# Slot weights without matmuls, four adaLN halves inside the router, one buffer for gathered rows and a 21st weight slot

## The chip, the core and the metric

The kernel runs on one core of a Trainium2 chip. The metric is the device time of one execution in microseconds, as the median of several runs. TensorE multiplies (its weight loads are counted apart, as PEld), VectorE and ScalarE do elementwise work and empty PSUM, GpSimd does almost nothing here, and SyncE (SP) issues nearly all DMAs, the weights among them.

## What is computed

The kernel computes two layers of a decoder trunk for 256 tokens of width 1024 in float32. Each layer has a mixer and a mixture of experts, both modulated by adaLN vectors made from a conditioning vector:

```python
c_act = jax.nn.silu(c)
for l in range(2):
    mod = c_act @ ada_w[l] + ada_b[l]
    sh1, sc1, gt1, sh2, sc2, gt2 = jnp.split(mod, 6, axis=-1)
    h = modulate(rms_norm(x, norm1_g[l]), sh1, sc1)
    x = x + gt1 * token_mixer(h, ...)      # retention, FoX, MLA; gates; out_w
    h = modulate(rms_norm(x, norm2_g[l]), sh2, sc2)
    x = x + gt2 * hier_moe(h, ...)
return rms_norm(x, final_g)
```

`hier_moe` picks for each token the best of 4 groups and the two best of its 8 experts, and adds the two results `(silu(xb @ w1[e]) * (xb @ w3[e])) @ w2[e]`, each by its weight. There are 32 experts, w1 and w3 of 1024 x 512 and w2 of 512 x 1024 each.

## The kernel before

The tokens are two tiles of 128 (index `t`), the width is two halves of 512 (index `n`). All weights come from HBM in loads of 1 MB (128 x 2048 float32). `Ring` holds the plan: the loads in a fixed order, each given to the first free slot (`fill`), and since one queue (SP, L139) issues them all, a load that has no free slot holds up those behind it. `take` hands out a loaded slot, `give` returns it, `grow` adds slots that live in memory that only one stage needs. There are 12 main slots (`slot`); during the experts 20: also two in `more_right`, three in `more_left`, and three in the work area `ar` (offsets `A_MORE`), of which the last is added when the mixer has ended.

The **mixer** computes adaLN vectors (`ada`), attention and gates, and last the out projection (`out`, L179 in `mm` as all matmuls, L188 is a transpose). An adaLN half (512 of its columns) is one load and is computed either as 16 passes of matmuls (out<-in of 32 x 512) or by VectorE (L511, then one matmul from `acc`). The halves' places in the plan are spread over the mixer; the last `ADA_TAIL` = 2 stand at its end, behind the out weights. `out` ends with the router: for each half `n`, VectorE adds the residual (`residual`, L592 and L593), `router_half` transposes x (L188), ScalarE copies it (L1224), and matmuls of 128 x 36 sum the logits. Then the left pool is opened, the last slot is added, two adaLN halves are computed (`ADA_FIRST`), and `route` runs: a chain of small VectorE operations per tile (`choose`, from L1251 on), with small matmuls in between (`pulse`) that have no use but to keep TensorE going.

The **experts** (`moe`) are taken in 16 pairs, 64 rows for each of the two (`CAP`), which fill the two halves of the 128 rows. `gather` picks their tokens by a matmul with a one-hot (`wanted`, L1320), into one of two buffers. A pair then runs on TensorE in this order: w1 (32 matmuls in two parts, each taking two loads), `combine` of the pair before (8 matmuls that add its rows to the tokens), `slots_of` (two one-hots transposed, and two matmuls of 128 x 2 that give each row its weight `wsl`; VectorE copies both out, L1372 and L1373), w3, the gather of the next pair around four transposes of the hidden rows (copied by ScalarE, L1436), w2. Each w2 half is scaled by `wsl` into `yh` and `yl`. If any expert has more than 64 tokens, `overflow` computes the rest; the test is a register load and a branch ahead of pair 12. In the last pair `gate_rows` spreads the gate's vector (two matmuls, two copies L583), and in layer 1 `final_gain` does the same for the final gain, a half each in pairs 11 and 12.

## Time and profile before

| | us |
|---|---|
| median of 3 runs | 1554.18 (1547.79, 1554.18, 1554.46) |
| the profiled execution | 1548.13 |
| its span | 1546.5 |
| TensorE busy in it | 1468.5 (95%) |
| VectorE, ScalarE busy | 661.7 (43%), 447.9 (29%) |
[...]

The span goes from the first to the last instruction; the profiled execution has its own time, which stands nearer to the lowest of the three runs. Layer 0's experts run from about 328 to 770 us, layer 1's from 1076 to 1527. PE is a TensorE matmul, PEld its weight load, DVE VectorE, ACT ScalarE, SPq the queue of SyncE. A time in a row is in microseconds from the span's start unless it is a mean of nanoseconds.

### The profile page before, as it was taken

The page shows a single profiled execution, that of the slowest core. Times are in us where ns is not written, and L with a number is a line of the kernel's source. Part 1 is how long each engine was busy: PE and PEld are TensorE (multiplying, and loading weights), DVE is VectorE, ACT ScalarE, POOL GpSimd, SP SyncE. Part 2 cuts the span into 40 slices and gives each one's busy share as a digit, 9 for nine tenths or more (in the row PEclk, how much of TensorE's full clock was granted, in tenths as well). Part 3 has the DMA queues.
Part 4 walks back from the last instruction along what each step waited for, and adds up shares of the span by engine and source line. Part 5 has one row for each costly group of instructions (what it writes and reads, how often), then busy time and mean ns, then how long its engine had stood idle before and what let it go on. Part 6 is the DMA issues. An engine that isn't in the chain of part 4 may idle for free. (4 is left out here: it accounts for less than half of the span.)

```text
span 1546.5 us, 21205 instructions
## 1 busy us (share of the span) xinstructions
PE 1468.5 (95%) x8326; PEld 897.6 (58%) x8326; DVE 661.7 (43%) x1756; ACT 447.9 (29%) x897; POOL 6.0 (0%) x10
## 2 busy tenths in 40 slices
PE   6898999999999999999989989999999999999996
PEld 3776889854444444444458679897444444444442
DVE  3766697962222222122157669767222222222223
ACT  3554534431111111111154454454211121111112
POOL 0000000000000000000000000000000000000001
PEclk9999999999999999999999999999999999999998
DMA  9963477998999999999995546668999999999993
GB/s 385 384 231 136 152 270 270 371 379 365 421 420 421 421 421 421 420 420 420 411 366 191 220 148 261 243 243 322 385 420 421 420 420 421 421 420 419 422 416 124
DMA packets 78542, 535.16 MB, mean 346 GB/s; under 512 B 8608, under 2 KB 8864, under 8 KB 15968
## 3 DMA queue, kind: packets, MB, share of 16 engines
q1 hardware_dynamic: 77776, 532.89, 85.2%
q8 instruction: 69, 1.13, 0.3%
q10 hardware_dynamic: 656, 0.80, 0.1%
q14 instruction: 41, 0.34, 0.1%
HBM read 532.61 MB, written 1.05 MB: 345 GB/s over the span
## 5 line engine op out<-in xcount | busy, mean ns | idle before, releaser
L179 PE MATMUL bank<-slot,ar 128*64 128x512 f32 (+1 forms) x1876 | 453.6, 593 | 1.8 <-ACT ar L1436 1.5
L179 PEld LDWEIGHTS bank<-slot,ar 128*64 128x64 f32 (+1 forms) x1876 | 143.0, 137 | 253.9 <-issue 235.6
L255 DVE TENSOR_TENSOR ws<-slot,ws 128x512 fp32r<-128x512 f32 (+1 forms) x276 | 186.5, 682 | 104.8 <-ACT ws L253 97.6
L179 PE MATMUL bank<-hr,ws 128*128 128x256 f32 x1536 | 204.7, 289 | 8.4 <-DVE ws L255 7.3
L179 PE MATMUL bank<-ar 128*64 128x512 f32 (+3 forms) x692 | 209.2, 502 | 0.7 <-DVE ar L885 0.7
L179 PEld LDWEIGHTS bank<-hr,ws 128*128 128x128 f32 x1536 | 191.8, 193 | 19.2 <-DVE ws L255 10.0
L253 ACT CAST ws<-slot 128x512 fp32r<-128x512 f32 (+1 forms) x276 | 164.4, 619 | 101.9 <-PE bank L179 95.8
L179 PE MATMUL bank<-ws,hr 128*128 128x512 f32 (+1 forms) x576 | 152.7, 410 | 10.0 <-ACT ws L253 4.6
L1338 ACT ACTIVATE ar<-bank,GS 128x128 f32<-128x128 f32 x128 | 58.6, 458 | 355.1 <-PE bank L179 324.3
L179 PE MATMUL bank<-more_left,ar 128*64 128x512 f32 x456 | 137.6, 594 | 0.0
L179 PEld LDWEIGHTS bank<-ar,x 128*128 128x128 f32 x1024 | 119.2, 192 | 25.1 <-issue 21.1
L179 PE MATMUL bank<-ar,x 128*128 128x128 f32 x1024 | 128.3, 278 | 1.7 <-DVE ar L1320 1.5
L179 PEld LDWEIGHTS bank<-ws,hr 128*128 128x128 f32 x576 | 107.7, 193 | 37.7 <-ACT ws L253 6.4
L1455 DVE SCALAR_TENSOR_TENSOR yl<-bank,wsl,yh 128x512 fp32r<-128x512 f32 x60 | 45.0, 750 | 157.6 <-ACT yh L1454 156.6
L179 PEld LDWEIGHTS bank<-ar 128*64 128x64 f32 (+2 forms) x692 | 80.9, 155 | 45.9 <-issue 38.1
L1372 DVE COPY wsl<-bank 64x1 f32<-64x1 f32 x64 | 10.0, 156 | 227.7 <-PE bank L179 227.2
L1336 DVE TENSOR_SCALAR ar<-bank,GS 128x128 f32<-128x128 f32 x128 | 52.5, 410 | 115.8 <-ACT ar L1338 115.8
L1419 DVE TENSOR_TENSOR R<-R,bank 128x512 f32<-128x512 f32 x32 | 22.0, 688 | 178.5 <-PE bank L179 178.5
L511 DVE SCALAR_TENSOR_TENSOR acc<-slot,cz,acc 128x512 f32<-128x512 f32 x122 | 90.8, 744 | 0.1
L179 PEld LDWEIGHTS bank<-more_left,ar 128*64 128x64 f32 x456 | 41.0, 137 | 82.5 <-issue 76.3
L1454 ACT ACTIVATE yh<-bank,wsl 128x512 fp32r<-128x512 f32 x60 | 41.3, 688 | 151.2 <-PE bank L179 151.2
L179 PE MATMUL bank<-yr,ws 128*128 128x256 f32 x576 | 75.4, 286 | 2.4 <-DVE ws L255 2.2
(244 smaller groups left out, 1158.8 us busy)
## 6 DMA issues: line engine op xcount, KB each, us to landing
slot<-in_exp_w SPq DMA_DIRECT2D x226, 1024.0 KB, 19.8
ar<-in_exp_w SPq DMA_DIRECT2D x54, 1024.0 KB, 19.8
more_left<-in_exp_w SPq DMA_DIRECT2D x54, 1024.0 KB, 19.8
slot<-in_ada_w SPq DMA_DIRECT2D x46, 1024.0 KB, 6.6
more_right<-in_exp_w SPq DMA_DIRECT2D x38, 1024.0 KB, 19.4
slot<-in_w_in SPq DMA_DIRECT2D x24, 1024.0 KB, 9.7
slot<-in_gate_w SPq DMA_DIRECT2D x23, 1024.0 KB, 5.0
slot<-in_branch_w SPq DMA_DIRECT2D x12, 1024.0 KB, 4.7
```

The lines of the kernel that those rows point to most:

```text
L179: self.nc.tensor.matmul(out, lhsT, rhs, start=start, stop=stop, skip_group_check=True)
L253: self.nc.scalar.copy(hi, w)
L255: self.nc.vector.tensor_tensor(lo, w, hi.bitcast(F32), ALU.subtract)
L511: nc.vector.scalar_tensor_tensor(acc, v[:, t, :], c, acc, ALU.mult, ALU.add)
L1336: nc.vector.tensor_scalar(hgT[:, j], pv[:, i], G[:, j:j + 1], S[:, j:j + 1], ALU.mult, ALU.add)
L1338: nc.scalar.activation(hgT[:, j], pv[:, i], AF.Identity, bias=S[:, j:j + 1], scale=G[:, j:j + 1])
L1372: nc.vector.tensor_copy(wsl(p)[es], ps[es, 256 + e:257 + e])
L1419: nc.vector.tensor_tensor(hid, hid, G[1], ALU.mult)
L1454: nc.scalar.mul(self.yp[n][0], G[n], wsl(p))
L1455: nc.vector.scalar_tensor_tensor(self.yp[n][1], G[n], wsl(p), self.yp[n][0].bitcast(F32), ALU.mult, ALU.subtract)
```

## The change

- `slots_of` has no 128 x 2 matmuls any more. The one-hots carry the weights, so the transposed rows hold the weight where they held 1; VectorE sums a row for `wsl` and compares with zero for the one-hot `OT`.
- The gathered rows have one buffer instead of two, the transposed hidden rows lie in `R`, the one-hots in `acc`. The memory that this frees is a fourth `A_MORE` slot, the 21st, added after `route`.
- `ADA_TAIL` and `ADA_FIRST` go from 2 to 4: four adaLN halves stand at the end of the mixer's plan. They are all matmuls and are computed inside `out`, between the two router halves. So fewer halves are left to VectorE.
- One `pulse` is gone. The rows of the second gate are copied before pair 0's Silu.
- The overflow test stands ahead of pair 11 in layer 0 and 13 in layer 1. `final_gain` runs in pair 13 and in the last pair, behind `gate_rows`. What only an overflow needs is done inside its branch.

```diff
-A_RV, A_RQK, A_RG, A_QT, A_KT, A_ST, A_RB = 0, 1024, 2048, 3072, 3584, 4096, 4096
+A_RV, A_RQK, A_RG, A_QT, A_KT, A_ST = 0, 1024, 2048, 3072, 3584, 4096
-A_HG, A_MORE, A_HIDT, A_OH = (4864, 5888), (0, 2048, 6912), 4096, (4608, 8960)
+A_HG, A_MORE = (4096, 8960), (0, 2048, 6912, 4864)
-ADA_TAIL, ADA_FIRST = 2, 2
+ADA_TAIL, ADA_FIRST = 4, 4
-OVERFLOW = 12
+OVERFLOW = (11, 13)
...
-        self.ring.grow([self.v(o, 2048) for o in A_MORE[:2]], l)
+        self.more = {o: self.v(o, 2048) for o in A_MORE}
+        self.ring.grow([self.more[o] for o in A_MORE[:2]], l)
...
                     if n:
                         self.finish(half)
+                        while not self.parked:
+                            self.step(self.live)
+                        self.tail = True
+                        for _ in range(ADA_FIRST):
+                            next(ga, None)
                     half = self.router_half(n)
...
         run(out())
-        while not self.parked:
-            self.step(self.live)
         pool = self.open_extra(l, "left", 3)
...
-        self.ring.grow([self.v(A_MORE[2], 2048)], l)
-        self.tail = True
-        for _ in range(ADA_FIRST):
-            next(ga, None)
+        self.ring.grow([self.more[A_MORE[2]]], l)
         self.route()
+        self.ring.grow([self.more[A_MORE[3]]], l)
...
         tsc(o1, self.iota0, fi[:, 0:1], None, ALU.is_equal)
-        self.pulse(t, o1)
...
-    def one_hot(self, p, t, by=None):
+    def one_hot(self, p, t, by):
-        oh = self.v(A_OH[t] + 2 * CAP * (p % 2), 2 * CAP)
+        c = 256 * t + 2 * CAP * (p % 2)
+        oh = self.acc[:, 0, c:c + 2 * CAP]
...
-            if by is None:
-                self.nc.vector.tensor_scalar(o, self.iota1[:, 0:CAP], r, None, ALU.is_equal)
-            else:
-                self.nc.vector.tensor_scalar(o, self.iota1[:, 0:CAP], r, by, ALU.is_equal, ALU.mult)
+            self.nc.vector.tensor_scalar(o, self.iota1[:, 0:CAP], r, by(e), ALU.is_equal, ALU.mult)
...
     def moe(self, l):
-        hg = [self.v(o, 8, 128) for o in A_HG]
+        hgT = [self.v(A_HG[0] + 128 * j if j < 6 else A_HG[1] + 128 * (j - 6), 128) for j in range(8)]
         hid = self.R
-        hidT = self.v(A_HIDT, 4, 128)
+        hidT = hid.rearrange("p (a b) -> p a b", a=4)
...
         def slots_of(p):
             ps = S[2]
-            oh = [self.one_hot(p, t) for t in range(NT)]
             for t in range(NT):
-                self.tr(ps[:, 128 * t:128 * t + 128], oh[t])
-            for t in range(NT):
-                self.mm(ps[:, 256:258], oh[t], self.W[:, t, 2 * p:2 * p + 2], t == 0, t == 1)
-            for e in range(2):
-                es = slice(64 * e, 64 * e + 64)
-                nc.vector.tensor_copy(wsl(p)[es], ps[es, 256 + e:257 + e])
-            nc.vector.tensor_copy(self.OT, ps[:, 0:256])
+                self.tr(ps[:, 128 * t:128 * t + 128], self.one_hot(p, t, lambda e: self.W[:, t, e:e + 1]))
+            nc.vector.tensor_reduce(wsl(p), ps[:, 0:256], AX.X, ALU.add)
+            nc.vector.tensor_scalar(self.OT, ps[:, 0:256], 0.0, None, ALU.not_equal)
...
-            if p == OVERFLOW:
+            if p == OVERFLOW[l]:
                 combine(p - 1)
-                self.overflow(l)
-            hgT = hg[p % 2]
+                self.overflow(l, hgT, lambda: self.gather(wanted(p), hgT))
...
             if p == 0:
                 self.together(self.rest)
+                R, vec = self.rowsB
+                self.rowsB = self.acc[:R.shape[0], 1], vec
+                nc.scalar.copy(self.rowsB[0], R)
...
-            if l == DEPTH - 1 and OVERFLOW - 1 <= p <= OVERFLOW:
-                self.final_gain(p - (OVERFLOW - 1))
+            if l == DEPTH - 1 and p == OVERFLOW[l]:
+                self.final_gain(0)
             if p == 0:
-                R, vec = self.rowsB
-                self.rowsB = self.acc[:R.shape[0], 1], vec
-                nc.scalar.copy(self.rowsB[0], R)
...
             elif end:
-                self.together(self.gate_rows(12 * l + 10, A_HG[0], self.rowsB, S[2:4]))
+                o = next(o for o in A_MORE if any(self.more[o] is s for s in self.ring.free))
+                self.together(self.gate_rows(12 * l + 10, o, self.rowsB, S[2:4]))
+                self.y32 = self.v(o + 1024, 1024)
+                if l == DEPTH - 1:
+                    self.final_gain(1)
```

On TensorE in layer 1, from the last transposes of the router's first half to the start of the choice (`bank_69` collects the logits, `bank_70` the adaLN vectors; `cz` is the conditioning vector), before:

```order
L188 MATMUL bank_67<-cst,x 128x128 x4
L179 MATMUL bank_69<-cst,ar 128x36 x8
L188 MATMUL bank_64<-cst,x 128x128 x4
L188 MATMUL bank_65<-cst,x 128x128 x4
L179 MATMUL bank_69<-cst,ar 128x36 x8
L179 MATMUL bank_70<-slot_92,cz 32x512 x4
L179 MATMUL bank_70<-slot_89,cz 32x512 x4
L179 MATMUL bank_63<-cst,sm 4x128
```

and now:

```order
L188 MATMUL bank_67<-cst,x 128x128 x4
L179 MATMUL bank_69<-cst,ar 128x36 x8
L179 MATMUL bank_70<-ar,cz 32x512 x8
L179 MATMUL bank_70<-slot_90,cz 32x512 x4
L179 MATMUL bank_70<-slot_100,cz 32x512 x4
L188 MATMUL bank_64<-cst,x 128x128 x4
L188 MATMUL bank_65<-cst,x 128x128 x4
L179 MATMUL bank_69<-cst,ar 128x36 x8
L179 MATMUL bank_63<-cst,sm 4x128
```

Two halves that stood behind the second set of logits, and two more, stand ahead of the transposes that lead to it.

On SP in layer 1, the expert loads around the end of the mixer (the two rows of `ar` are the first `A_MORE` slots, `more_left` the left pool), before:

```order
L139 DMA slot_98<-in_exp_w 128x2048
L139 DMA slot_100<-in_exp_w 128x2048
L139 DMA ar<-in_exp_w 128x2048 x2
L139 DMA more_left_7358<-in_exp_w 128x2048
L139 DMA more_left_7359<-in_exp_w 128x2048
L139 DMA more_left_7360<-in_exp_w 128x2048
L139 DMA ar<-in_exp_w 128x2048
L139 DMA slot_92<-in_exp_w 128x2048
L139 DMA slot_89<-in_exp_w 128x2048
```

and now:

```order
L139 DMA slot_91<-in_exp_w 128x2048
L139 DMA slot_97<-in_exp_w 128x2048
L139 DMA ar<-in_exp_w 128x2048 x2
L139 DMA slot_90<-in_exp_w 128x2048
L139 DMA slot_100<-in_exp_w 128x2048
L139 DMA more_left_7346<-in_exp_w 128x2048
L139 DMA more_left_7347<-in_exp_w 128x2048
L139 DMA more_left_7348<-in_exp_w 128x2048
L139 DMA ar<-in_exp_w 128x2048 x2
```

The four slots ahead of the left pool are now those of the four adaLN halves, and behind the pool two loads go to `ar` instead of one.

On TensorE in a pair of layer 1, from the last matmul of a combine to w3 (`bank_69` takes the transposed one-hots, `bank_64` w3), before:

```order
L179 MATMUL bank_68<-yh_7364,OT 128x512
L179 MATMUL bank_68<-yl_7365,OT 128x512
L188 MATMUL bank_69<-cst,ar 128x128 x2
L179 MATMUL bank_69<-rt,ar 128x2 x2
L179 MATMUL bank_64<-slot_91,ar 64x512
```

and now:

```order
L179 MATMUL bank_68<-yh_7352,OT 128x512
L179 MATMUL bank_68<-yl_7353,OT 128x512
L188 MATMUL bank_69<-cst,acc 128x128 x2
L179 MATMUL bank_64<-more_left_7346,ar 64x512
L179 MATMUL bank_64<-more_left_7347,ar 64x512
```

The pair of matmuls from `rt`, which holds the weights, is gone.

## Rows read from the trace of the kernel before

**Rows 1.** The page's first part: busy us, share of the span, instructions.

```profile
PE 1468.5 (95%) x8326; PEld 897.6 (58%) x8326; DVE 661.7 (43%) x1756; ACT 447.9 (29%) x897; POOL 6.0 (0%) x10
```

**Rows 2.** Stretches: from:to, length, busy PE, PEld, DVE, ACT, POOL, clock, DMA share, GB/s.

```profile
1375.00:1400.00 25.00, 25.00 (x136) 12.08 (x136) 6.11 (x18) 4.28 (x8) 0.00 (x0) 1.00 1.01 420
...
321.50:390.50 69.00, 65.53 (x366) 33.11 (x367) 21.77 (x107) 14.68 (x30) 0.00 (x0) 0.95 0.95 390
...
1068.90:1133.40 64.50, 61.86 (x360) 31.35 (x360) 22.14 (x107) 15.79 (x33) 0.00 (x0) 1.00 0.97 399
...
341.40:348.30 6.90, 6.48 (x18) 2.68 (x20) 2.31 (x12) 0.48 (x1) 0.00 (x0) 0.51 1.00 411
```

**Rows 3.** The chain of waits, pairs 13 to 15 of layer 1: start, us.

```profile
1454.49 0.22 PE bank L188 x2
...
1482.35 0.22 PE bank L188 x2
...
1520.22 0.59 ACT ar L1436
```

**Rows 4.** Issues on SP, one load each: start, us, line.

```profile
314.67 0.33 SPq L139 DMA_DIRECT2D slot<-in_exp_w  x1
...
736.76 0.33 SPq L139 DMA_DIRECT2D slot<-in_exp_w  x1
...
1064.29 0.33 SPq L139 DMA_DIRECT2D ar<-in_exp_w  x1
...
1479.39 0.33 SPq L139 DMA_DIRECT2D slot<-in_exp_w  x1
```

**Rows 5.** The same four loads in that order: KB each, us from issue to landing.

```profile
slot<-in_exp_w SPq DMA_DIRECT2D x1, 1024.0 KB, 6.8
...
slot<-in_exp_w SPq DMA_DIRECT2D x1, 1024.0 KB, 19.8
...
ar<-in_exp_w SPq DMA_DIRECT2D x1, 1024.0 KB, 4.6
...
slot<-in_exp_w SPq DMA_DIRECT2D x1, 1024.0 KB, 20.3
```

**Rows 6.** TensorE in time, pair 15 of layers 0 and 1: start, us, count.

```profile
763.48 0.50 PE L179 MATMUL bank<-yh,OT 128*128 128x512 f32 x1
...
1508.08 0.50 PE L179 MATMUL bank<-yh,OT 128*128 128x512 f32 x1
...
1510.26 0.51 PE L179 MATMUL bank<-rt,ar 128*128 128x2 f32 x4
1510.69 0.65 PE L179 MATMUL bank<-slot,ar 128*64 128x512 f32 x2
```

**Rows 7.** The page's groups: busy us, mean ns, idle before and its releaser.

```profile
L1372 DVE COPY wsl<-bank 64x1 f32<-64x1 f32 x64 | 10.0, 156 | 227.7 <-PE bank L179 227.2
```

**Rows 8.** TensorE and VectorE in time, from mixer to experts, layer 1.

```profile
1063.71 2.79 PE L179 MATMUL bank<-ws,hr 128*128 128x512 f32 x11 [0.23 <-DVE ws L255]
...
1066.78 1.92 PE L179 MATMUL bank<-cst,ar 128*128 128x36 f32 x16
...
1071.95 1.93 PE L179 MATMUL bank<-slot,cz 128*32 128x512 f32 x16
1072.48 0.42 DVE L1251 SCALAR_TENSOR_TENSOR ar<-bank,rs,sb 128x36 f32<-128x36 f32 x2
...
1076.41 4.21 PE L179 MATMUL bank<-ar,x 128*128 128x128 f32 x32 [0.76 <-DVE ar L1320]
1080.54 7.09 PE L179 MATMUL bank<-slot,ar 128*64 128x512 f32 x32
```

**Rows 9.** The same in layer 0: last output matmuls and start of the choice.

```profile
313.44 2.79 PE L179 MATMUL bank<-ws,hr 128*128 128x512 f32 x11 [0.23 <-DVE ws L255]
...
323.66 0.42 DVE L1251 SCALAR_TENSOR_TENSOR ar<-bank,rs,sb 128x36 f32<-128x36 f32 x2
```

**Rows 10.** TensorE in time, pair 12 of layer 1: a final gain.

```profile
1433.09 1.12 PE L179 MATMUL bank<-adab,cst 32*128 32x512 f32 x2
```

## The prediction

> **What bounds the kernel now.** I read the page first, then stretches, then the chain, and last the expert loads one by one. On the page TensorE is busy 95% of the span and VectorE 43% [rows 1], which says that TensorE is the bound. A stretch says that there is a second one as close: in 25 us in the middle of the experts TensorE is busy all 25 us at full clock, and the DMA engines are full too, at 420 GB/s [rows 2]. One weight load is 1 MB (1,048,576 bytes), so at that pace one lands every 2.49 us, and a pair of experts (12 loads) costs the transfers 29.9 us. TensorE needs less: the chain of waits, in which it stands alone, repeats from pair to pair after 27.86 us (1454.49, 1482.35) [rows 3]. TensorE therefore gains 2 us per pair on the transfers and lives on what was loaded ahead; the question is whether that stock lasts to the last pair.

> It does, barely. The last large loads before the end of a layer are those of pair 15. In layer 0 the second half of its w1 is issued at 736.76 [rows 4] and takes 19.8 us [rows 5], so it lands at 756.6. The 32 matmuls of a w1 take 7.09 us [rows 8] and end where the combine begins, at 763.48 [rows 6], so the second half begins at 763.48 - 3.55 = 759.9: **3.4 us** to spare. In layer 1: issued 1479.39, 20.3 us, landed 1499.7, used at 1508.08 - 3.55 = 1504.5: **4.8 us** to spare. So both sides have to be summed in each layer, what TensorE gains or loses until there, and by how much the loads shift. The later of the two decides.

> [...]

> **TensorE in the pairs.** The slot weights no longer come from matmuls. Before, the passes with the 128x2 operand begin at 1510.26, behind the two transposes, and w3 follows at 1510.69 [rows 6]. Without them w3 would follow the transposes: 0.43, say 0.44 us per pair, 16 pairs, **-7.0 us a layer**. VectorE does a little more (a second operation in each one-hot, a sum and a comparison instead of two copies and a cast). I count it as nothing: it waited 227.2 us for TensorE ahead of the 64 old copies, 7 us a pair [rows 7], and the result is read at the end of w2, over 15 us later. Nor does the one buffer for gathered rows cost anything: its next writer is the gather behind w3, in TensorE's own order.

> **TensorE between mixer and experts.** The four last adaLN halves (all matmuls now) move in between the router's first 128x36 matmuls and the transposes of its second half. Two such halves take 1.93 us in layer 1, 0.96 each, and they ran behind the router, beside VectorE's choice of experts. Now 3.86 us stand ahead of the transposes. In layer 1 the last output matmul ends at 1063.71 + 2.79 = 1066.50 and the choice starts at 1072.48, 6.0 us later [rows 8]. I put it at 9.3 to 9.4: 3.86 more, less 0.5 since the residual is then long done and the transposes run without a break. **+3.4 us.** The two halves that leave their old place give nothing back, because the choice hid them. In layer 0 the output ends at 313.44 + 2.79 = 316.23 and the choice starts at 323.66, 7.4 later [rows 9], because VectorE still has adaLN sums to do ahead of the residual. These sums go, so layer 0 becomes like layer 1: 9.3 after the output, **+1.8 us**.

> **TensorE elsewhere.** The overflow test moves from pair 12 to pair 11 or 13 and costs the same there: no term. One of the two final gains, **1.1 us** [rows 10], no longer stands ahead of pair 15's w1 in layer 1. It comes back at the end: its matmul has to wait for the bank of the second gate copy, and its own copy of some 0.6 us goes ahead of the copy at 1520.22 that releases the last w2 [rows 3]. That is 0 if both run in the shade of the transposes and 1.7 if none does; I take **+1.4 us**, since the gate copies end when the transposes do, and little shade is left.

> TensorE alone: layer 0, +1.8 - 7.0 = -5.2; layer 1, +3.4 - 7.0 - 1.1 + 1.4 = -3.3; together -8.5.

> **The loads.** Two more slots hold adaLN halves at the end of the mixer, so only 12 expert loads are out before the router instead of 14; the 13th waits for the first of the halves, and the three of the left pool stand behind them on SP, which issues in order. The first half is through 3.1 us after the output (1066.78 + 1.92 + 0.96 = 1069.6, [rows 8]). A load that finds the queue empty takes 4.6 us, as the one issued at 1064.29, the 14th of layer 1, which landed at 1068.9 [rows 4, 5]. In layer 1 the 13th would then land at 1074.2 and the 14th at 1076.7, **7.8 us later** than before. In layer 0 the 13th would land at 316.23 + 3.1 + 4.6 = 323.9; before it was issued at 314.67 and took 6.8, so 321.5: **2.4 us later**. From there transfers still had gaps before: a DMA share of 0.95 over 69.0 us in layer 0 and 0.97 over 64.5 us in layer 1 [rows 2], so 3.5 and 1.9 us idle. They are idle for want of a free slot. The stream is now later against TensorE and has a 21st slot, so I take it that these gaps close: a shift of 2.4 - 3.5 = **-1.1** and 7.8 - 1.9 = **+5.9**. The late ends are the gaps coming back in full, +2.4 and +7.8. The early ends are a stream at 420 GB/s instead of the 390 and 399 of those rows: 69.0 x 30/420 = 4.9 and 64.5 x 21/420 = 3.2, so -2.5 and +4.6.

> **The sum.** Layer 0, second half of pair 15's w1: by the loads -1.1 - 3.4 = -4.5, by TensorE +1.8 - 15 x 0.44 = -4.8. The later is -4.5; one more 0.44 makes the layer's end **-4.9**. Layer 1 starts earlier by that much. There, by the loads +5.9 - 4.8 = +1.1, by TensorE +3.4 - 6.6 - 1.1 = -4.3. The loads decide: +1.1 - 0.44 + 1.4 = **+2.1**. Together -2.8 us. With the early ends -5.2 (TensorE decides) and +0.8, so -4.4; with the late ones -1.4 and +4.0, so +2.6. The profiled execution took 1548.13 us (span 1546.5, 1.6 around it), so it would be 1545.3. The three runs lie at two levels, 1547.79 and 1554.2 to 1554.5, and the profile is at the lower one; on their median 1554.18 the forecast is **1551.4 us**, with bounds 1549.8 and 1556.8. A measurement of this kernel can tell about 0.5% (7.8 us) from no change; the forecast lies within.

> **Rivals.** First, *the loads are not the bound*: the stock is larger than I count, because more than those gaps close. Then TensorE's sum holds, -8.5: 1545.7 us. The half-clock stretch in layer 0, 6.9 us at a granted clock of 0.51 from 341.40 with TensorE busy 6.48 [rows 2], which is half of that too long, 3.2 us, may go as well, since the work ahead of it moves: -11.7, 1542.5. For it: the 21st slot is one load, 2.49 us, of stock. Against it: only 12 loads are out before the router, and layer 1 would need 5.4 us more than I find.

> Second, slower: *the clock falls to its lower level in the route*. The halves that ran beside the choice leave it, and TensorE has little to do until the gather at 1076.41, 3.9 us after the choice's start (1.4 us of those halves filled it [rows 8]). [...] It decides only if the fall comes before w1, not behind it as in layer 0 now. Against it: layer 0's fall is the only one in a route, and layer 1 has the full clock from 1068.90 on [rows 2]. [...]

> Third, *the 21st slot brings nothing*: it is granted after the route and lets SP run ahead only where DMA is full anyway; the gaps come back: +2.6, 1556.8 us.

> **How the numbers follow.** Forecast 0.52; loads no bound 0.22; clock 0.12 (half of it both layers); slot without effect 0.14. The range leaves out the clock in both layers, part of it in layer 0 alone, and what the first rival may bring beyond the gain of the clock: from 1542.5 to 1558. Faster by over 0.5% is most of the first rival, and part of the forecast if the runs settle at the lower of the two levels: 0.27. Slower is the clock: 0.09. The rest, 0.64, lies within.

> **What would show it.** In the profile after: w3 directly behind the transposes; the choice 9.3 us after the last output matmul in both layers; the 14th load of layer 1 landing 10 us after the output, and full DMA from there to the end; TensorE waiting for a load in pair 14 or 15 of layer 1, which before has no such wait in its chain; the last w2 1.4 us later behind w3. I am wrong if pair 15 of layer 1 finds its loads landed for over 2 us (then -8.5), if the granted clock is 0.5 ahead of a first w1, or if the stream of loads has new gaps behind the 14th.

## The result: 0.8% slower

The changed kernel takes **1565.55 us** (median of 6 runs, 1560.25 to 1566.44) against 1551.16 for the kernel before (median of 6): ratio 1.0084, 95% interval 1.0065 to 1.0104. The prediction was 1551.4 with a range up to 1558.0; the measured time lies above it, on the side that had a chance of 0.09.

The two spans differ by 17.8 us, and 5.4 of that is not the change: the runs of both kernels lie at two levels 5 to 6 us apart, the profile of before is from the lower and that of after from the upper, and level against level the change is 12 to 13 us. What differs is TensorE's granted clock in the first 70 us (a mean of 0.95 before and 0.90 after), here in two rows of the stretches (columns as in [rows 2]), the kernel before and the changed kernel:

```profile
48.00:54.00 6.00, 4.97 (x22) 3.97 (x23) 3.56 (x9) 3.77 (x8) 0.00 (x0) 1.00 1.00 415
```

```profile
48.00:54.00 6.00, 4.39 (x12) 3.22 (x13) 3.60 (x9) 4.22 (x9) 0.00 (x0) 0.66 1.00 418
```

The changed kernel with another place for its tests (first experiment) had the full clock there and a first mixer of 315.8 us, and it has the same code up to there, so the code does not decide it. Without these 5.4 us the traces differ by 12.4.

The page of the changed kernel, the line that answers to [rows 1]:

```profile
PE 1470.5 (94%) x8222; PEld 891.1 (57%) x8222; DVE 659.8 (42%) x1708; ACT 447.6 (29%) x897; POOL 6.8 (0%) x10
```

TensorE has 104 matmuls less and is not less busy, and the span has grown by more than its busy time. From the same marks in both traces, in us:

| | layer 0 before | after | layer 1 before | after |
|---|---|---|---|---|
| mixer, to the last output matmul | 316.2 | 321.6 | 280.9 | 279.8 |
| from there to the choice | 7.4 | 9.7 | 6.0 | 9.7 |
| choice to gather | 3.9 | 3.9 | 3.9 | 3.9 |
| first gather | 4.1 | 6.2 | 4.1 | 6.6 |
| pair 0 | 33.6 | 30.5 | 27.3 | 27.0 |
| pairs 1 to 15 | 420.3 | 423.3 | 422.1 | 426.2 |

The last line is the surprise. Nearly every pair is 0.34 us shorter, and yet the sum is longer. The waits of TensorE in the changed kernel, layer 0 and then layer 1 (us in total, times, longest):

```profile
PE bank L179 <- PEq L1480: 6.1, 1, 6.1
PE bank L179 <- DMA more_left<-in_exp_w: 5.9, 1, 5.9
```

Both stand directly behind the overflow test, at pair 11 and at pair 13. TensorE in time there:

```profile
649.40 0.40 PE L179 MATMUL bank<-yl,OT 128*128 128x512 f32 x1
655.87 6.55 PE L179 MATMUL bank<-slot,ar 128*64 128x512 f32 x17 [6.08 <-PEq L1480]
...
1454.72 0.40 PE L179 MATMUL bank<-yl,OT 128*128 128x512 f32 x1
1461.05 6.73 PE L179 MATMUL bank<-slot,ar 128*64 128x512 f32 x17 [5.93 <-DMA more_left<-in_exp_w]
```

The second is put down to a load by inference only: the two loads that its first matmuls need had landed by 1446.6, 14 us earlier. What takes the time is the branch of the test itself, on TensorE's sequencer (two branches, ns: least, median, most), before and now:

```profile
L1482 PEldq COMPARE_BRANCH x2: 446/454/462, 674.0 to 1417.5; - x2
...
L1480 PEldq COMPARE_BRANCH x2: 6068/6124/6180, 649.4 to 1454.6; - x2
```

In both, 17 matmuls then take 6.6 to 6.7 us, where 16 such matmuls take 3.65 behind the test of the kernel before (at 674.80), which has no stop. That is the clock: it is granted at 0.50 for the first 5 us behind the stop.

```profile
655.87:660.90 5.03, 5.03 (x12) 1.61 (x14) 0.82 (x4) 0.00 (x0) 0.00 (x0) 0.50 1.02 419
...
1461.00:1466.00 5.00, 4.95 (x12) 1.64 (x14) 0.86 (x4) 0.00 (x0) 0.00 (x0) 0.50 1.01 416
```

Against the shift of the pairs around them the tests cost 8.1 and 8.3 us more than in the kernel before, **16.4 in all**: about 6 us each of standing still and over 2 of half clock. The DMA queues from 650 to 656 us (packets, MB, share) show what goes on in the first stop: one 16 KB transfer of the instruction queue. It begins at 652.99 and takes 1.1 us; the branch ends at 655.49, 2.5 us after the transfer's start. In the second stop a transfer begins at 1458.24 and the branch ends at 1460.74, 2.5 us again.

```profile
q1 hardware_dynamic: 333, 2.44, 99.4%
q8 instruction: 1, 0.02, 1.1%
```

### The profile page after: what moved, and what is told of

It is laid out like the page before. It is cut to its first block, busy times and chain, and to the rows that moved or that the text cites. A ratio compares the mean times of both kernels' runs of the same rounds, so it can differ in the third digit from the quotient of the medians.

```text
span 1564.3 us, 20965 instructions
## 1 busy us (share of the span) xinstructions
PE 1470.5 (94%) x8222; PEld 891.1 (57%) x8222; DVE 659.8 (42%) x1708; ACT 447.6 (29%) x897; POOL 6.8 (0%) x10
## 3 DMA queue, kind: packets, MB, share of 16 engines
HBM read 532.61 MB, written 1.05 MB: 341 GB/s over the span
## 4 chain that ended last, share of the span: by engine, by line
PE 46%; DVE 6%; DMA 4%; ACT 2%; issue 1%; DVEq 0%; ACTq 0%; SPq 0%
PE bank L179 44%; DMA slot<-in_exp_w 3%; DVE ws L255 1%; PE bank L188 1%; DMA more_left<-in_exp_w 1%; DVE acc L511 1%; ACT ws L253 0%; ACT ar L662 0%; DVE x L1384 0%; DVE ar L1383 0%; DVE R L1383 0%; ACT ar L990 0%; DVE sm L210 0%; DVE sm L661 0%; DVE ar L667 0%
## 5 line engine op out<-in xcount | busy, mean ns | idle before, releaser
L179 PE MATMUL bank<-slot,ar 128*64 128x512 f32 (+2 forms) x1192 | 341.5, 602 | 12.0 <-PEq L1480 6.1
L179 PEld LDWEIGHTS bank<-slot,ar 128*64 128x64 f32 (+1 forms) x1192 | 105.8, 140 | 183.0 <-issue 166.4
L179 PE MATMUL bank<-slot,R 128*64 128x512 f32 x616 | 178.2, 596 | 1.3 <-ACT R L1434 1.3
L179 PE MATMUL bank<-ar 128*64 128x512 f32 (+4 forms) x616 | 176.3, 489 | 0.7 <-DVE ar L885 0.7
L179 PE MATMUL bank<-ws,hr 128*128 128x512 f32 (+1 forms) x576 | 156.0, 417 | 10.2 <-ACT ws L253 4.6
L179 PEld LDWEIGHTS bank<-acc,x 128*128 128x128 f32 x1024 | 124.2, 198 | 24.9 <-issue 21.9
L179 PE MATMUL bank<-acc,x 128*128 128x128 f32 x1024 | 133.0, 285 | 1.5 <-DVE acc L1319 1.5
L1366 DVE TENSOR_REDUCE wsl<-bank 128x1 f32<-128x256 f32 x32 | 13.6, 425 | 214.2 <-PE bank L188 214.2
L179 PEld LDWEIGHTS bank<-slot,R 128*64 128x64 f32 x616 | 53.7, 137 | 77.3 <-issue 71.1
L179 PE MATMUL bank<-more_left,ar 128*64 128x512 f32 x296 | 96.3, 596 | 0.0
L511 DVE SCALAR_TENSOR_TENSOR acc<-slot,cz,acc 128x512 f32<-128x512 f32 x108 | 80.4, 744 | 0.0
## 6 DMA issues: line engine op xcount, KB each, us to landing
slot<-in_exp_w SPq DMA_DIRECT2D x216, 1024.0 KB, 19.8
ar<-in_exp_w SPq DMA_DIRECT2D x68, 1024.0 KB, 19.8
more_left<-in_exp_w SPq DMA_DIRECT2D x52, 1024.0 KB, 19.8
more_right<-in_exp_w SPq DMA_DIRECT2D x36, 1024.0 KB, 19.8
```

What stands on the lines that cost most here:

```text
L179: self.nc.tensor.matmul(out, lhsT, rhs, start=start, stop=stop, skip_group_check=True)
L511: nc.vector.scalar_tensor_tensor(acc, v[:, t, :], c, acc, ALU.mult, ALU.add)
L1366: nc.vector.tensor_reduce(wsl(p), ps[:, 0:256], AX.X, ALU.add)
```

## The experiments

The question was first why the test costs 6 us where it cost nothing, then what the adaLN tail and the clock cost, and last whether the loads would decide once the stops are gone.

**The tests at pairs 7 and 9.**

```diff
-OVERFLOW = (11, 13)
+OVERFLOW = (7, 9)
```

> The changed kernel with its overflow tests ahead of pairs 7 and 9 instead of 11 and 13; nothing else. In the trace of the changed kernel TensorE stood still 6.1 us behind the test in layer 0 and 5.9 in layer 1, and a 16 KB transfer of the instruction queue (8) began in each stop (653.0, 1458.2). Behind the last such transfer TensorE had begun 181 and 193 instructions when it came to the test; in the kernel before 30 and 30, and there was no stop. Theory J (the jump over the overflow code lands in instructions that have not been fetched, and how far the last fetch lies back decides): pairs 7 and 9 of the changed kernel stand 30 and 26 instructions behind a transfer, so no stop over 1 us, 6 to 8 us less in each layer, 12 to 15 us less in all: about 1551. With the loads on the edge (1 us to spare in pair 15 by the shift) up to 2 us of this may be given back. Rival L (the overflow code has grown by a gather, so every jump is longer than what is fetched ahead, wherever it stands): both stops stay at about 6 us, and the time stays within 2 us of the changed kernel's 1565.

Measured: 1561.53 us, ratio 1.0078 (1.0057 to 1.0099). Both stops are still there:

```profile
PE bank L179 <- PEq L1480: 12.2, 2, 6.2
```

So the way back to the last transfer does not decide alone, and rival L stood.

**slots_of alone**, on the kernel before, with its test at 12:

```diff
...
-            oh = [self.one_hot(p, t) for t in range(NT)]
             for t in range(NT):
-                self.tr(ps[:, 128 * t:128 * t + 128], oh[t])
-            for t in range(NT):
-                self.mm(ps[:, 256:258], oh[t], self.W[:, t, 2 * p:2 * p + 2], t == 0, t == 1)
-            for e in range(2):
-                es = slice(64 * e, 64 * e + 64)
-                nc.vector.tensor_copy(wsl(p)[es], ps[es, 256 + e:257 + e])
-            nc.vector.tensor_copy(self.OT, ps[:, 0:256])
+                self.tr(ps[:, 128 * t:128 * t + 128], self.one_hot(p, t, lambda e: self.W[:, t, e:e + 1]))
+            nc.vector.tensor_reduce(wsl(p), ps[:, 0:256], AX.X, ALU.add)
+            nc.vector.tensor_scalar(self.OT, ps[:, 0:256], 0.0, None, ALU.not_equal)
```

> The kernel before with the new slots_of alone (weights by the transposed one-hots, no 128x2 matmuls). Test at pair 12, overflow code as before. TensorE's gain by the trace of the changed kernel is 0.34 us a pair, 10.9 us in 32 pairs. Each pair is 8 TensorE instructions shorter, so the test at pair 12 stands some 190 instead of 30 instructions behind the last instruction transfer. Theory J: a stop of about 6 us behind both tests, so 0 to +3 us against the kernel before. Rival L (long overflow code): no stop, and 8 to 11 us faster than before. A third, the loads decide (20 slots, 3.4 and 4.8 us to spare in pair 15 of layers 0 and 1, used up by 5.4 us of gain a layer): waits for loads of 1 to 2 us in pair 15, so 2 us less gain.

Measured: 1545.29 us, ratio 0.9964 (0.9950 to 0.9978). Each pair is 0.34 us shorter. In layer 0 TensorE stops at the branch. In layer 1 it doesn't, but 5 us behind the branch it waits 1.4 us for "issue", and the pair is 2.0 us longer for it:

```profile
681.24 1.12 PE L179 MATMUL bank<-more_right,ar 128*64 128x512 f32 x2 [6.10 <-PEq L1474]
...
1421.07 1.51 PE L179 MATMUL bank<-slot,ar 128*64 128x512 f32 x6 [0.30 <-PEq L1474]
...
1426.49 2.79 PE L179 MATMUL bank<-slot,ar 128*64 128x512 f32 x12 [1.38 <-issue]
```

The code behind the test is as long as before here, so its growth is not needed for a stop either. **The kernel before with its test at pair 11:**

```diff
-OVERFLOW = 12
+OVERFLOW = 11
```

> The kernel before with its test ahead of pair 11 instead of 12 (the final gains move along, to pairs 10 and 11). Its pair 11 stands 228 and 227 instructions behind the last instruction transfer, pair 12 30 and 30. Theory J: a stop of several us behind the test in both layers, 8 to 14 us slower than before. Rival L: no stop, within 2 us of before.

Measured: 1566.88 us in one run, both layers stop:

```profile
PE bank L179 <- PEq L1482: 12.3, 2, 6.3
```

One pair earlier costs the kernel before 17.5 us against the median beside it (9.0 and 8.6 in the two pairs of the test), more than the whole change. Both conditions together fit all that had run: the number of instructions that TensorE began since the last instruction transfer, plus the length of the jump. The jump is 443 instructions in the kernel before and 509 in the changed one, which gathers the pair's rows again behind an overflow. For the places that were run, counted from the traces (which lack a few records) and the compiled instruction streams; "stop" is one at the branch, "small" a wait that begins 3.5 to 5 us behind it, with what it adds to the pair:

```
                        layer 0: since + jump        layer 1: since + jump
kernel before            30 + 443 = 473  no stop       31 + 443 = 474  no stop
changed kernel          183 + 509 = 692  stop         196 + 509 = 705  stop
tests at 7 and 9         46 + 509 = 555  stop          47 + 509 = 556  stop
slots_of alone          185 + 443 = 628  stop          51 + 443 = 494  small, 2.0 us
before, test at 11      247 + 443 = 690  stop         251 + 443 = 694  stop
short code              183 + 333 = 516  small, 2.6   264 + 333 = 597  stop
short code, pulse       187 + 333 = 520  small, 2.7    31 + 333 = 364  no stop
short code, old tail    157 + 333 = 490  no stop       79 + 333 = 412  no stop
slots_of, test at 8      46 + 443 = 489  small, 2.2    47 + 443 = 490  small, 1.9
```

In these places nothing was lost up to 474, and from 555 on TensorE stood at the branch each time. From 489 to 520 it passed the branch, and in five of six places it waited a little later; the counts are too rough to order the places in this band. (The two last versions below keep the old tail and its places and lose at most 0.4 us there.) Between two transfers TensorE begins 252 to 256 instructions (means over the experts in three traces), so two transfers are some 510. The price of a stop is about 6 us of standing and over 2 of half clock in this kernel. The small waits end like the stops at the branch: 2.4 to 2.5 us after a 16 KB transfer begins (in the last row at 566.11 and 1416.70, for transfers from 563.64 and 1414.29). That TensorE waits for the instructions in these transfers is my reading of the times; what they hold, and why they begin when they do, no run shows.

**Shorter code behind the test**, the tests where the change has them. The two blocks of rows are a loop on the chip instead of being written out:

```diff
-                for b in range(2):
...
+                with tc.For_i(0, 2, 1):
...
```

> The changed kernel with its tests at 11 and 13 as they are; only the code behind the test is shorter, its two blocks being a loop on the chip instead of written out. By the built programs TensorE's jump over it goes 333 instructions ahead instead of 509 (443 in the kernel before). The runs so far fit one rule: no stop where the way from the point at which the last instruction transfer began to the jump's target is 473 to 494 instructions (the kernel before, layer 1 of the run with slots_of alone), a stop of 6 us where it is 555 or more (all others); two transfers of 256 would be 512. Here it is some 503 in layer 0, on the edge, and 350 in layer 1. Rule holds: no stop in layer 1, 7 to 8 us less than the changed kernel there; in layer 0 none or the same 6 us; so 1550 to 1558. If the place or the growth of other code decides: both stops stay, within 2 us of 1565. Where TensorE gets so early that the loads of pair 15 decide, up to 1 us is given back as a wait for a load in layer 1.

Measured: 1555.83 us, ratio 1.0031 (1.0013 to 1.0050). It came out with the layers as in the table: only the small wait in layer 0, on the edge, and a stop in layer 1, where I had expected none, since the transfer that I counted from came only after the test (264 instructions back is the one before). TensorE in time, layer 0 and layer 1:

```profile
649.43 3.62 PE L179 MATMUL bank<-slot,ar 128*64 128x512 f32 x14 [0.30 <-PEq L1480]
654.82 1.17 PE L179 MATMUL bank<-slot,ar 128*64 128x512 f32 x4 [1.76 <-issue]
...
1454.91 6.10 PE L179 MATMUL bank<-slot,ar 128*64 128x512 f32 x17 [5.79 <-PEq L1480]
```

In layer 0 TensorE passes the branch, runs 14 matmuls and then waits for "issue" until 2.4 us after a transfer that begins at 652.41. No half clock follows: the next 4 matmuls take 1.17 us, where 4 behind a stop (tests at 7 and 9, at 540.05) take 1.97. **The same with the removed pulse back:**

```diff
         tsc(o1, self.iota0, fi[:, 0:1], None, ALU.is_equal)
+        self.pulse(t, o1)
```

> The run with the short code, plus the pulse that the change removed from the choice of experts. If its absence lets the clock fall ahead of the first gather, the gather takes 4.2 us in both layers at full clock instead of 6.3 and 6.4; if the adaLN halves' new place is the cause, it stays near 6.3. The tests stand as in the run with the short code (within 8 instructions).

Measured: 1554.81 us in one run. With the pulse's instructions ahead of the test layer 1 has no stop: the transfer now begins just ahead of it, by 31 instructions. With the halves where the change has them the pulse does not help the clock: the first gather takes 6.1 and 6.5 us.

**slots_of alone, layer 0's test at pair 8:**

```diff
-OVERFLOW = 12
+OVERFLOW = (8, 12)
...
```

> The kernel before with the new slots_of alone, as in the earlier run, but the test of layer 0 ahead of pair 8 instead of 12 (layer 1 stays at 12). By the rule the way is 469 and 494 instructions, so no stop in either layer. The earlier run stood still 6.1 us in layer 0 and was 0.36% faster than before. Rule holds: 6 to 7 us less than that run, about 10 to 12 us faster than before, 1538 to 1540; in layer 1 the second half of pair 15's w1 had 0.6 us to spare there, so a wait for a load of up to 1 us may show. Rule fails: as the earlier run, 1545.

Measured: 1543.00 us, ratio 0.9963 (0.9948 to 0.9979). TensorE no longer stands at the branch, so the rule held there, and pairs 1 to 15 of layer 0 take 417.4 us instead of 423.2. But the small wait is in both layers:

```profile
566.11 0.65 PE L179 MATMUL bank<-ar 128*64 128x512 f32 x2 [1.62 <-issue]
...
1416.70 2.79 PE L179 MATMUL bank<-slot,ar 128*64 128x512 f32 x12 [1.22 <-issue]
```

The two pairs are 2.2 and 1.9 us longer for it, and there the expected 1538 to 1540 was missed: of the 10.9 us that 32 shorter pairs give, 6.8 are left, and the spans of the two traces, 1546.5 before and 1540.3 here, differ by 6.2. So 489 to 494 is not free, as I had taken it to be. Against the earlier run's trace, layer 0's pair 0 took 1.6 us more (33.4 for 31.8; 33.6 in the kernel before, with the half-clock stretch of [rows 2]) and layer 1's mixer 0.7 more, which gives 2.3 of the 5.8 us back; the ratio is that of the earlier run (0.9964), so this gain is shown by the traces and not by the medians.

**The adaLN tail undone**, with the short code and tests at stop-free places (11 and 10):

```diff
-ADA_TAIL, ADA_FIRST = 4, 4
+ADA_TAIL, ADA_FIRST = 2, 2
...
-                        for _ in range(ADA_FIRST):
-                            next(ga, None)
...
+        self.tail = True
+        for _ in range(ADA_FIRST):
+            next(ga, None)
         self.route()
```

> As the last one, with the adaLN tail undone: two halves at the end of the plan instead of four, computed behind the router as in the kernel before, and the tests at pairs 11 and 10, 475 and 456 instructions by the rule, so without a stop. In the trace of the changed kernel the four halves cost the start of the choice 2.3 us in layer 0 and 3.6 in layer 1, and the gather behind it ran at half clock for 2.0 and 2.3 more. If the adaLN halves' place is the cause of both, the choice starts 6.0 to 7.4 us behind the output as before and the gather takes 4.2 us: 6 to 9 us less than the changed kernel would take without stops, so 1541 to 1545. If the half clock is not from the halves' place but from the missing pulse or from chance, it stays: 4 us less of that. If the loads decide, the two more loads ahead of the router make up 5 us and pair 15 does not wait.

Measured: 1540.42 us, ratio **0.9936** (0.9916 to 0.9957), just under the expected 1541 to 1545. The choice starts 7.4 and 6.0 us behind the output, as before. The first gather takes 4.1 us in layer 0 but 5.8 in layer 1, at a clock of 0.72 over the stretch. **With the pulse back and the last final gain behind the copy of the hidden rows:**

```diff
+        self.pulse(t, o1)
...
             nc.scalar.copy(hidT.rearrange("p a b -> p (a b)"), ps)
+            if end and l == DEPTH - 1:
+                self.final_gain(1)
```

> The run with the short code and the adaLN tail undone, plus two small things: the pulse that the change removed is back, and the last final gain is issued behind the copy of the hidden rows instead of ahead of it. In that run layer 1's first gather took 5.8 us instead of 4.1 and the last pair lost 1.9 us between w3 and w2. If the missing pulse let the clock fall there, the gather takes 4.1 to 4.2 us in both layers, 1.6 us less; if the fall is chance, 5.8 again. The last w2 should start 1.5 to 1.9 us earlier behind w3, about 10.2 us instead of 12.1. Together 2 to 3.5 us less than 1540.4: 1537 to 1538.5. Pair 15 had 1.1 and 0.9 us to spare, so in layer 1 up to 1 us may come back as a wait for a load.

Measured: 1537.63 us, ratio **0.9912** (0.9882 to 0.9942), the fastest of all. The gathers in layer 1, first without and then with the pulse:

```profile
1071.42 5.83 PE L179 MATMUL bank<-acc,x 128*128 128x128 f32 x32 [0.76 <-DVE acc L1319]
```

```profile
1074.49 4.21 PE L179 MATMUL bank<-acc,x 128*128 128x128 f32 x32 [0.76 <-DVE acc L1320]
```

The last w2 begins 10.7 us behind w3 instead of 12.1, a little less of a gain than expected (10.2).

**The 21st slot.** It was taken away twice, with and without the stops:

```diff
-        self.ring.grow([self.more[A_MORE[3]]], l)
```

> The changed kernel with tests at 7 and 9 and without the 21st slot. If the loads decide as in the prediction: pair 15 in layers 0 and 1 waits for loads, 1 to 4 us in all, and the time is that much above the run with the slot. If TensorE decides with more to spare: no wait for a load and within 1 us of it.

Measured beside the tests at 7 and 9: 1562.08 us in one run against 1561.53, no wait for a load. The second half of pair 15's w1 has 6.7 and 6.0 us to spare instead of 9.9 and 7.7.

> The same without the 21st slot (its memory holds the last gate rows). With the tests' stops in place the slot moved the landing of pair 15's w1 by 3.2 us in layer 0 and 1.7 in layer 1 and nothing waited. Now, without stops, there is about 1 us to spare with the slot. If the loads come to decide, as the prediction had it: waits for loads of 1 to 3 us in layer 0 and up to 2 in layer 1, so 1 to 4 us slower than with the slot. If TensorE still decides: no wait, within 1 us of it.

Measured beside the fastest version: 1540.65 us, ratio to the kernel before 0.9943 (0.9924 to 0.9962). Now the load is late. Pair 15's w1 in layer 0:

```profile
752.19 4.51 PE L179 MATMUL bank<-slot,ar 128*64 128x512 f32 x18
757.08 3.65 PE L179 MATMUL bank<-slot,ar 128*64 128x512 f32 x14 [0.38 <-DMA slot<-in_exp_w]
```

It begins at 752.19 and ends at 760.7, 8.5 us instead of 7.1: 1.4 us are lost there and 0.6 in layer 1, 2.0 in the trace; the medians say 3.0 with overlapping intervals. With the slot the spare is 1.4 and 1.9 us and nothing waits.

## Point by point

**The test: "costs the same there: no term".** This step failed: the stops cost 16.4 us, of a miss of 15.2 by the traces (+12.4 for the forecast -2.8) and 17.2 by the medians (+14.4). I compared the work at the test, which is the same, and not the jump. The kernel before shows the jump only as a gap of nothing (branches of 446 and 462 ns), with its test 30 and 31 instructions behind a transfer. Moving the test by one pair is enough for the stop, as the kernel before with its test at 11 shows. So are the 66 instructions by which the code between branch and target had grown: 46 to 51 instructions behind a transfer, a jump of 443 passes the branch and one of 509 stops at it. Neither changes what any engine computes.

**slots_of, 0.44 us a pair.** Right in kind, too large: 0.34. Before, w3 began 0.65 us after the transposes, and without the 0.43 of the passes [rows 6] it would be 0.22; it is 0.31. In the changed kernel:

```profile
1433.86 0.38 PE L188 MATMUL bank<-cst,acc 128*128 128x128 f32 x2
1434.17 7.09 PE L179 MATMUL bank<-slot,ar 128*64 128x512 f32 x32
```

In 32 pairs that is 10.9 instead of 14.0. VectorE's part was free, as said: among TensorE's waits none on the new sum or comparison shows.

**The router, 9.3 to 9.4 us to the choice.** Nearly right: 9.7 in both layers (here layer 1, answering to [rows 8]; the output ends at 1075.0).

```profile
1072.17 2.83 PE L179 MATMUL bank<-ws,hr 128*128 128x512 f32 x11 [0.22 <-DVE ws L255]
...
1077.12 1.92 PE L179 MATMUL bank<-ar,cz 128*32 128x512 f32 x16
1078.86 1.90 PE L179 MATMUL bank<-slot,cz 128*32 128x512 f32 x16
1080.69 1.10 PE L188 MATMUL bank<-cst,x 128*128 128x128 f32 x8
...
1084.66 0.42 DVE L1253 SCALAR_TENSOR_TENSOR ar<-bank,rs,sb 128x36 f32<-128x36 f32 x2
1085.46 1.31 PE L179 MATMUL bank<-cst,sm 128*4 128x128 f32 x8 [1.25 <-DVE sm L1262]
...
1088.59 6.69 PE L179 MATMUL bank<-acc,x 128*128 128x128 f32 x32 [0.75 <-DVE acc L1319]
1095.21 7.09 PE L179 MATMUL bank<-slot,ar 128*64 128x512 f32 x32
```

**The clock, the second rival.** It came in part: the gather ran slow, not w1, in both layers, with a granted clock of 0.62 and 0.60 over these stretches.

```profile
334.00:342.00 8.00, 7.16 (x39) 6.44 (x40) 4.11 (x27) 3.51 (x10) 0.00 (x0) 0.62 1.01 421
...
1088.00:1096.00 8.00, 7.41 (x36) 6.75 (x38) 3.66 (x20) 3.25 (x10) 0.00 (x0) 0.60 1.01 419
```

That cost 2.0 and 2.5 us; the old half-clock stretch behind w1 in layer 0 [rows 2] went, 2.7 back. Over the runs: in the five traces with the halves inside the router the first gather takes 6.1 to 6.2 us in layer 0 and 5.6 to 6.7 in layer 1, with or without the pulse; with the halves behind the router it takes 4.1 in layer 0 in all seven. In layer 1 the pulse seems to be needed as well: 4.1 in the six traces with it, 5.8 in the only one without. So in these traces the clock held where the halves ran beside the choice, in layer 1 with the pulse besides; TensorE was busy 2.89 us between choice and gather in layer 1 before and 1.58 in the changed kernel. "Against it", the absence of a fall in layer 1 of the kernel before, was weak evidence, because there the halves filled that very stretch. A first w1 at half clock, which this rival's chance counted with, did not come: it takes 7.09 us in both layers of the changed kernel. The clock also fell where no rival had it, to 0.50 behind the two stops.

**The loads.** Their shift was right: in the changed kernel the second half of pair 15's w1 is issued at

```profile
741.46 0.33 SPq L139 DMA_DIRECT2D slot<-in_exp_w  x1
...
1492.97 0.33 SPq L139 DMA_DIRECT2D slot<-in_exp_w  x1
```

and takes 19.8 us both times, so it lands at 761.3 and 1512.8. Less what the layer's own mixer moved (5.4 and 8.5) that is -0.7 and +4.6, where I had -1.1 and +5.9 with an early end of +4.6. That the loads *decide* was wrong here, since the stops put TensorE behind them by 8.7 and 8.5 us (the sign that I named for the first rival, and not for its reason), and nearly right for the kernel without stops: the run with the short code and the pulse has 3.0 and 0.5 us to spare. The third rival, the 21st slot without effect, fell: it is worth 1.7 to 3.2 us of landing and, where nothing else hides it, 2 us of time by the trace (the intervals of the medians overlap).

**The final gain.** 1.05 us per pair as said, and 1.9 instead of 1.4 at the end: the transposes waited too, a little over the text's 1.7 for no shade at all. The chain of that pair, where before stood [rows 3]:

```profile
1536.82 1.12 PE L179 MATMUL bank<-adab,cst 32*128 32x512 f32 x2 [0.68 <-ACT ar L583]
1537.87 0.66 PE L188 MATMUL bank<-cst,R 128*128 128x128 f32 x4
...
1538.56 0.58 ACT L1434 COPY R<-bank 128x512 f32<-128x512 f32 x1
1539.20 4.08 PE L179 MATMUL bank<-slot,R 128*64 128x512 f32 x17 [0.67 <-ACT R L1434]
```

**The sum redone.** TensorE's own -8.5, plus 16.4 for the stops and the half clock behind them, 3.1 for the smaller gain in slots_of, 1.8 for the clock at the gathers (2.0 + 2.5 - 2.7), 0.7 for the router, 0.5 for the last pair, and -1.1 for a shorter mixer in layer 1, is +12.9. The traces say +12.4 without the first mixer, the medians +14.4.

What stays open: why layer 1's mixer is 1.1 us shorter, what sets the clock in the first 70 us from run to run, and why of two places at 490 one waits and the other does not.

## What to carry to other kernels

Code that is jumped over can still cost time: in layer 0 a jump of 509 instructions cost 8.1 us at the same place where one of 333 cost 2.6. Keep such code short (a loop on the chip instead of written-out blocks), and after any change that adds or removes instructions look behind each branch in the trace for a stop that no load explains. Filler work beside a sparse chain can earn its place by the clock of what follows (the first gather went from 4.1 us to 6.2 and 6.6 here), so moving it out may have a price beyond its own time. And where two bounds lie within a few us, sum both, since whichever edit removes the nearer one makes the other decide.
